# Chunk solves of a gated DeltaNet layer moved out of the step-by-step recurrence, output products in a stream of their own, PSUM banks shared anew

## The chip, the core and the metric

The kernel runs on one core of a Trainium2 chip. The metric is the device time of one execution in microseconds (us), from profiled or timed runs. TensorE (PE) multiplies into PSUM, eight banks of 128 x 512 float32; VectorE (DVE) and ScalarE (ACT) read PSUM; GpSimd (POOL) works on SBUF alone; SyncE (SP) issues the DMAs. Each engine takes its instructions in the order in which the program put them into its queue.

## The reference, cut to what matters

A block of two layers over 512 tokens (256 context, 256 latent), width 2048. Layer 0 is a bidirectional chunked gated DeltaNet, layer 1 differential attention. The part of layer 0 that is changed, for every head, direction and chunk:

```python
lower = jnp.where(strict, jnp.einsum('nbhid,nbhjd->nbhij', kb, kc) * decay, 0.0)
tinv = lax.linalg.triangular_solve(eye + lower, ...)          # per chunk
u = tinv @ (vc * bc[..., None])
w = tinv @ (kb * jnp.exp(gc)[..., None])
a_intra = jnp.einsum('nbhid,nbhjd->nbhij', qc, kc) * decay

def step(s, inp):
    q_i, k_i, u_i, w_i, a_i, gl_i = inp
    v_new = u_i - w_i @ s
    o_i = q_i @ s + a_i @ v_new
    s = s * gl_i[..., None, None] + jnp.einsum('bhck,bhcv->bhkv', k_i, v_new)
    return s, o_i
```

The kernel takes chunks of 128 tokens: four chunks (two of context, two of latent tokens), 32 value heads in 16 groups of two heads that share a key head, two directions.

## The kernel before

Layer 0 projects the normalised tokens to q, k, two v and two z tiles for each group g: six projections of 16 x 3 matmuls (three, because each float32 operand is split into a high part and a low part). A projection's weights come as four DMAs of 256 KB into `raw` tiles (four buffers), are split by ACT (`hi`) and POOL or DVE (`lo`) in `split` (L185, L187), and the products gather in a `pj` bank. The names in the traces say which: `g6z0hi` is the high part of group 6, first z projection.

The rest of layer 0 runs beside these projections. A planner written in the kernel (`Drive`, L497) holds a set of streams, Python generators, each with a priority, and lets the first one that is ready emit its next instructions; a stream says how much TensorE time it has just emitted and how long its result will take, and waits for events (`ev`) or for counted resources (`res`: `pj` 2, `kT` 3, `qT` 3, `v` 3, `m` 4, `uf` 8, `at` 3, and so on). The projections are the `filler`, with the lowest priority. The streams are:

- `stream_m`: per group and half (two chunks) the matrix of the triangular system in float16 plus a bfloat16 rest (`m16`, `ml`), and the inverse of its 16 x 16 diagonal blocks on DVE (`block_inv`);
- `stream_lev` (two): three levels that join the blocks into `uf`, an approximate inverse per chunk, by chains `iv` matmul, `R` on DVE (L783), `iv` matmul, `T` and `U` on ACT (L800, L801);
- `stream_at`: the masked, decayed scores `at`;
- `stream_b`: the recurrence, four steps per group, each with both directions and both heads. A step (`steps_b`, L849 to L933) multiplies the state with the keys (`sb` from `S` and `kT`), forms `y` on DVE (L874), casts it (L879), applies `uf`, casts (L898), multiplies by `m16` and `ml`, forms the rest on DVE (L905), applies `uf` again and adds (L911): that is the solve of the chunk with one refinement. Then come the new state (`sb` from `x` and `kx`, L918 or L921) and the outputs (`so` from `S` and `qT`, `so` from `x` and `at`), and `chain_fin` normalises and transposes the outputs of a half.

The eight PSUM banks are `pj` 2, `tr` 1, `iv` 2, `gq` 1, `sb` 1, `so` 1. On POOL and ACT runs besides the work on the modulation weights (`ada_pieces`: `rp` on L138, L139), fed by the DMAs `aw` and `cr`. After the streams follow the output projection in two halves (`woA`, `woB`), layer 1 (`dv`, `dk`, `dq`, `dg`) and its output projection (`dwo`), which use the same `raw` tiles; the products for q and the gate (`dq`, `dg`) and `dwo` have 256 columns, the others 512.

Of the kernel before, what the change touches and what calls it, by code (L numbers as in the profile page):

```python
# [20 lines left out]
P = 128  # L21
# [40 lines left out]
def body(ctx, tc, D, d, out):  # L62
# [87 lines left out]
    def ada_pieces(lcs):  # L150
# [3 lines left out]
        for q in range(NQ):  # L154
            yield
            cr = wp.tile([P, 2, NK], F32, name=f"cr{lcs[0]}{q}", tag="cr", bufs=2)
# [71 lines left out]
    sc_d = dram.tile([2, D], F32, name="sc_d")  # L228
    mb_d = [dram.tile([8, US], F16, name=f"mb_d{i}") for i in range(2)]
# [22 lines left out]
    gq = lambda: pt_("gq", 1)  # L252
# [4 lines left out]
    def so():  # L257
        return psm.tile([P, 2, 2, P], F32, tag="so", name="so", bufs=1)
# [37 lines left out]
    for k0 in range(0, KT, SK):  # L296
        with tc.high_priority():
            for kind in range(2):
                if k0 + kind:
                    pr = kind * HKT + k0 // 2  # L300
                    ada_pair(0, pr, ada_load(0, pr, t0, "ar", 12), (gq, tr)[np_ % 2](), t0)
                np_ += 1
# [24 lines left out]
    lv = cst.tile([P, 3, P], F32, name="lv")  # L327
    nc.sync.dma_start(lv, d["consts"][:, C_LV + 4 * P:C_LV + 7 * P].rearrange("p (l i) -> p l i", l=3))
# [27 lines left out]
    zt = dl.tile([P, 1024], F16, name="zt", tag="m16", bufs=4)  # L356
# [9 lines left out]
    hh = lambda kt: hhi[:, kt, :]  # L366

# [7 lines left out]
    def gates():  # L375
        class t1:
            @staticmethod
            def tile(shape, dt, name, tag, bufs=2):
                return dl.tile(shape, dt, name="gt_" + name, tag=tag, bufs=dict(at=3, x=1, cy=1, jk=1, y=1, grm=1, gra=1, ma=1).get(tag, bufs))
# [53 lines left out]
        g = t1.tile(sh, F32, name="g", tag="x")  # L433
# [121 lines left out]
    def post_k(g, ps):  # L555
# [8 lines left out]
        kT = dl.tile([P, NCH, P], F32, tag="kT", name=f"kT{g}", bufs=3)  # L564
        kt_ = dl.tile([P, NCH, P], F32, tag="ktok", name=f"ktok{g}", bufs=3)
        pt = tr()
# [9 lines left out]
        for c in range(NCH):  # L576
            nc.scalar.activation(kt_[:, c], pt[:, c * P:(c + 1) * P], AF.Copy, scale=rk[:, c:c + 1])
        yield 0.87, 6.0 * LX
        pt2 = tr()
# [3 lines left out]
        sts[g].update(kT=kT, ktok=kt_)  # L583
        yield 0.87, 1.5 * LX
        dr.set("kT", g)

    def post_q(g, ps):
# [13 lines left out]
        yield 0.0, 9.0 * LX  # L601
        pq = tr()
# [5 lines left out]
        dr.set("rq", g)  # L608
        yield 0.85, 0.0
# [13 lines left out]
    def post_v(g, h, ps):  # L623
        if h == 0:
            yield ("v", 2)
            sts[g]["v"] = [dl.tile([P, 2, 2, P], F32, tag="v", name=f"v{g}{i}", bufs=3) for i in range(2)]
# [9 lines left out]
        v = sts[g]["v"]  # L636
        pv = tr()
# [4 lines left out]
        for i in range(2):  # L642
            nc.scalar.activation(v[i][:, :, h, :], pvv[:, 2 * i:2 * i + 2], AF.Copy, scale=0.5)
        yield 0.87, 2.0 * LX
# [47 lines left out]
    def scaled(o, gr, pg, s, nm):  # L692
        gm = dl.tile([P, 2, P], F32, tag="gm", name=f"gm{s}{nm}", bufs=1)
        nc.vector.tensor_tensor(gm, pg.unsqueeze(1).to_broadcast([P, 2, P]), gam[:, s], ALU.mult)
# [3 lines left out]
    def block_inv(g, half, m16):  # L698
# [8 lines left out]
        TU = dl.tile([64, 2, 16, 16], F16, tag="bT", name=f"bT{nm}", bufs=1)  # L707
# [15 lines left out]
    def stream_m():  # L723
        for g in range(G):
            yield ev("kT", g)
            kT = sts[g]["kT"]
            for half in range(2):
# [6 lines left out]
                m16 = dl.tile([P, 2, 2, 2, P], F16, tag="m16", name=f"m16{nm}", bufs=4)  # L734
                ml = dl.tile([P, 2, 2, 2, P], BF16, tag="ml", name=f"ml{nm}", bufs=4)
                pg = gq()
                for k in range(2):
                    c = 2 * half + k
                    mm(pg[:, k * P:(k + 1) * P], kT[:, c], kT[:, c])
                for k in range(2):  # L740
# [3 lines left out]
                    scaled(ma, gr, pg[:, k * P:(k + 1) * P], 0, f"{g}{c}")  # L744
# [7 lines left out]
                free("gq", 1, 14)  # L752
                yield 0.44, 12.0 * LX

    def stream_lev(p):
        yield ev("conv", 0, "v0")
        yield ev("conv", 0, "v1")
        for g in range(G):
            for half in range(2):
# [17 lines left out]
                for n in range(4, 7):  # L777
# [10 lines left out]
                    if last:  # L788
                        uf = dl.tile([P, 4, P], F16, tag="uf", name=f"uf{g}{c}", bufs=8)
# [14 lines left out]
    def stream_at():  # L804
        for g in range(G):
# [4 lines left out]
            for half in range(2):  # L810
# [3 lines left out]
                for k in range(2):  # L814
                    c = 2 * half + k
                    mm(pg[:, k * P:(k + 1) * P], st["kT"][:, c], st["qT"][:, c])
                for k in range(2):
# [3 lines left out]
                    scaled(at, gr, pg[:, k * P:(k + 1) * P], 1, f"{g}{c}")  # L821
                    st["at"][c] = at
                dr.set("at", g, half, lat=8.0 * LX)
                free("gq", 1, 14)
                yield 0.44, 8.0 * LX

    def stream_b():
        if "k1" in early:
            yield ev("conv", 1, "k")
        for g in range(G):  # L830
            st = sts[g]
            for h in range(2):
                yield ev("v", g, h)
            S = dl.tile([P, 2, 2, P], F32, tag="S", name=f"S{g}", bufs=1)
            for half in range(2):
                for k in range(2):
                    yield ev("uf", g, 2 * half + k)
                O = dl.tile([P, 2, 2, P], F32, tag="O", name=f"O{g}{half}", bufs=2)
                for t in (2 * half, 2 * half + 1):
                    yield from steps_b(g, t, half, st, S, O)  # L840
                free("m")
                free("uf", 2)
                free("v")
                free("at", 2)
                dr.add(2, chain_fin(g, half, O))
            free("kT")
            free("qT")

    def steps_b(g, t, half, st, S, O):  # L849
        kT, qT, ktok, uf = st["kT"], st["qT"], st["ktok"], st["uf"]  # L850
        v = st["v"][half]
        m16, ml = st["m"][half]
        cd = (ORDER[0][t], ORDER[1][t])
        col = lambda a, dd, h: a[:, cd[dd], dd, 2 * g + h:2 * g + h + 1]
        fl = lambda a: a.rearrange("p d h i -> p (d h i)")
        f2 = lambda a: a.rearrange("p h i -> p (h i)")
        DH = [(dd, h) for dd in range(2) for h in range(2)]

        def vec(tag, dt=F32):
            return dl.tile([P, 2, 2, P], dt, tag=tag, name=f"{tag}{g}{t}", bufs=1)  # L860
# [7 lines left out]
        if t > 0:  # L868
            b = sb()
            for dd in range(2):  # L870
                mm(f2(b[:, dd]), kT[:, cd[dd]], f2(S[:, dd]))
            y = vec("y")
            for dd, h in DH:
                nc.vector.scalar_tensor_tensor(y[:, dd, h], b[:, dd, h], col(eg, dd, h), v[:, cd[dd] % 2, h],  # L874
                                               ALU.mult, ALU.subtract)
        else:
            y = v
        yb = vec("yb", BF16)
        nc.scalar.copy(fl(yb), fl(y))  # L879
        if t > 0:  # L880
            o1 = so()
            for dd in range(2):
                mm(f2(o1[:, cd[dd] % 2]), qT[:, cd[dd]], f2(S[:, dd]))
            for dd, h in DH:
                c = cd[dd] % 2
                if t == 2:
                    nc.scalar.activation(O[:, c, h], o1[:, c, h], AF.Copy, scale=col(eg, dd, h))
                else:
                    nc.vector.scalar_tensor_tensor(O[:, c, h], o1[:, c, h], col(eg, dd, h), O[:, c, h],
                                                   ALU.mult, ALU.add)  # L890
# [404 lines left out]
```

## Time and profile before

| what | value |
|---|---|
| median of three timed runs | 3165.09 us (3162.82 to 3166.16) |
| the profiled execution, its own time | 3170.24 us |
| its span, first to last instruction | 3168.5 us |
| TensorE busy, share of the span | 89% |
| VectorE, ScalarE, GpSimd busy | 62%, 59%, 64% |
| mean granted clock of TensorE | 0.954 of full speed |

A busy share is an average over stages: start-up to about 240 us, the streams of layer 0 beside the projections to about 2060 us, the output projection to about 2440 us, then layer 1. A matmul's time in the trace reaches from its start to its modelled end, and matmuls overlap; the distance from start to start tells what one costs in a dense row.

### The profile page before, as it was taken

To read this page: it belongs to the slowest core of one execution; us is meant where nothing else is said; L and a number is where in the kernel's file an instruction comes from. 1 tells how busy PE (TensorE), PEld (TensorE's weight loads), DVE (VectorE), ACT (ScalarE), POOL (GpSimd) and SP (SyncE) were. 2 spreads that over 40 slices of the span, in tenths; PEclk is the share of its full clock that TensorE was granted. 3 is DMA by queue.
4 is the path that set the end of the run, shared out by engine and by line. 5 is a ranking of instruction groups with operands and counts; after the bars stand their busy time and mean duration, and the time that the engine had idled before them with its cause. 6 is when DMAs were issued, how large, how long until landed. Compare 5 with 4: busy or idle time off the path is not lost.

```text
span 3168.5 us, 52448 instructions
## 1 busy us (share of the span) xinstructions
PE 2833.0 (89%) x16178; PEld 2236.6 (71%) x16178; DVE 1980.1 (62%) x4274; ACT 1863.0 (59%) x5466; POOL 2026.2 (64%) x2370
## 2 busy tenths in 40 slices
PE   4977888888998988998988988899898999999998
PEld 1555666676776766776766766677686888888888
DVE  2148768778778688588688688632334664545454
ACT  3545666666766766766666666654455665434354
POOL 2567677777787777777777777566466677322234
PEclk6988999999999999999999999999999999999999
DMA  9645445455545555545455546656744454333345
GB/s 362 223 114 118 123 119 135 123 133 118 139 134 129 127 126 133 128 129 136 122 125 131 132 118 134 173 171 189 230 147 132 144 164 150 123 110 113 117 127 164
DMA packets 511795, 457.06 MB, mean 144 GB/s; under 512 B 241684, under 2 KB 383764, under 8 KB 511508
## 3 DMA queue, kind: packets, MB, share of 16 engines
q1 hardware_dynamic: 511508, 453.68, 51.8%
q8 instruction: 127, 2.08, 0.3%
q14 instruction: 156, 1.28, 0.1%
q10 hardware_dynamic: 4, 0.02, 0.0%
HBM read 427.18 MB, written 26.36 MB: 143 GB/s over the span
## 4 chain that ended last, share of the span: by engine, by line
PE 33%; DVE 26%; DMA 19%; ACT 7%; POOL 7%; issue 5%; SPq 2%; POOLq 0%; DVEq 0%; ACTq 0%
PE pj L83 28%; DMA gra<-gc_d 5%; POOL rp L138 4%; DMA grm<-gc_d 4%; DVE bP L712 4%; DVE grm L687 3%; DMA aw<-in_adaw_dram 3%; DVE gra L687 2%; DVE bY L714 2%; ACT rp L139 2%; DVE R L783 1%; PE sb L83 1%; DMA ar<-in_adaw_dram 1%; PE iv L83 1%; DVE ma L695 1%
## 5 line engine op out<-in xcount | busy, mean ns | idle before, releaser
L139 ACT ACTIVATE rp<-rp 128x256 f32<-128x256 f32 x1024 | 426.9, 417 | 378.6 <-POOL rp L138 375.5
L712 DVE TENSOR_TENSOR bP<-bX,bY 64x1 f32<-64x1 f32 (+14 forms) x480 | 228.8, 477 | 18.1 <-ACT bY L710 9.8
L139 ACT ACTIVATION_READ_ACCUMULATOR rp<-rp 128x1 f32 x1024 | 194.0, 189 | 0.0
L687 DVE TENSOR_SCALAR gra<-gra,gct,lnb 128x128 f32<-128x128 f32 x256 | 114.3, 488 | 97.9 <-DMA gra<-gc_d 97.2
L687 DVE TENSOR_SCALAR grm<-grm,gct,lnb 128x128 f32<-128x128 f32 x256 | 144.9, 610 | 47.9 <-DMA grm<-gc_d 47.3
L783 DVE TENSOR_TENSOR R<-iv,lv 128x512 f16<-128x512 f32 x192 | 126.1, 678 | 32.8 <-PE iv L83 32.6
L689 ACT ACTIVATE grm<-grm 128x512 f32<-128x512 f32 x64 | 40.4, 631 | 132.0 <-DVE grm L687 127.1
L83 PEld LDWEIGHTS <-m 128*128 128x128 f16 x1024 | 74.2, 100 | 62.0 <-issue 57.7
L714 DVE TENSOR_REDUCE bY<-bP 64x1 f32<-64x1 f32 (+14 forms) x480 | 108.8, 227 | 8.7
L83 PE MATMUL iv<-U,R 128*128 128x128 f16 x768 | 75.7, 223 | 34.4 <-DVE R L783 30.0
L83 PEld LDWEIGHTS <-R 128*128 128x128 f16 x768 | 47.6, 99 | 77.6 <-DVE R L783 44.6
L745 POOL TENSOR_TENSOR ma<-ma,cs 128x512 f32<-128x512 f32 x64 | 85.3, 1333 | 20.7 <-DVE ma L695 18.3
L83 PE MATMUL sb<-yb,uf 128*128 128x128 bf16 x512 | 54.2, 225 | 40.7 <-ACT yb L879 22.2
L689 ACT ACTIVATE gra<-gra 128x512 f32<-128x512 f32 x64 | 40.4, 631 | 84.1 <-DVE gra L687 84.1
L83 PE MATMUL iv<-T,m 128*128 128x128 f16 x768 | 71.4, 223 | 15.8 <-ACT T L800 7.2
L224 DVE TENSOR_TENSOR hlo<-mh,hhi 128x512 fp32r<-128x512 f32 x32 | 29.6, 929 | 86.8 <-ACT hhi L223 77.8
L748 POOL TENSOR_TENSOR ml<-ma,m 128x512 bf16<-128x512 f32 x64 | 76.1, 1189 | 10.5 <-ACT m L747 10.3
L83 PEld LDWEIGHTS <-uf 128*128 128x128 f16 x512 | 36.4, 100 | 64.6 <-issue 59.1
L801 ACT CAST U<-iv 128x512 f16<-128x512 f32 x128 | 75.7, 591 | 0.0
L800 ACT CAST T<-iv 128x512 f16<-128x512 f32 x128 | 73.7, 576 | 3.0 <-PE iv L83 2.9
L83 PE MATMUL so<-x,at 128*128 128x128 f32 x512 | 71.6, 280 | 3.8 <-DVE x L911 2.7
L83 PEld LDWEIGHTS so<-x,at 128*128 128x128 f32 x512 | 64.9, 194 | 6.2 <-DVE x L911 3.6
(2758 smaller groups left out, 11429.3 us busy)
## 6 DMA issues: line engine op xcount, KB each, us to landing
aw<-in_adaw_dram SPq DMA_DIRECT2D x512, 128.0 KB, 3.0
ar<-in_adaw_dram SPq DMA_DIRECT2D x64, 512.0 KB, 7.3
gra<-gc_d SPq DMA_DIRECT2D x128, 128.0 KB, 4.2
grm<-gc_d SPq DMA_DIRECT2D x128, 128.0 KB, 4.1
mb_d<-m SPq DMA_DIRECT2D x32, 256.0 KB, 3.7
T<-tu_d SPq DMA_DIRECT2D x128, 64.0 KB, 2.7
U<-tu_d SPq DMA_DIRECT2D x128, 64.0 KB, 2.7
yd<-sz SPq DMA_DIRECT2D x32, 256.0 KB, 3.4
```

The costliest lines, as they stand in the source:

```text
L83: nc.tensor.matmul(o, l, r, start=start, stop=stop)
L138: nc.gpsimd.tensor_tensor(pr, r, cr[:, s], ALU.mult)
L139: nc.scalar.activation(pr, pr, AF.Copy, accum_out=acc[:, s, q:q + 1])
L687: nc.vector.tensor_scalar(gr[:, u], gr[:, u], gct[:, c, dd, j:j + 1], lnb[:, c, dd, j:j + 1], ALU.subtract, ALU.min)
L689: nc.scalar.activation(gr, gr, AF.Exp)
L712: nc.vector.tensor_tensor(pr[:, :i, :i], X[:, i, :i].unsqueeze(1).to_broadcast([64, i, i]), Y[:, :i, :i].rearrange("p j c -> p c j"), ALU. ...
L714: nc.vector.tensor_reduce(Y[:, i, :i], pr[:, :i, :i], AX.X, ALU.add)
L745: nc.gpsimd.tensor_tensor(ma, ma, ident.unsqueeze(1).to_broadcast([P, 4, P]), ALU.add)
L748: nc.gpsimd.tensor_tensor(ml[:, :, k], mv, m16[:, :, k], ALU.subtract)
L783: nc.vector.tensor_tensor(R, quad(pp), lvb(n), ALU.mult)
L800: nc.scalar.copy(Tm, quad(pt))
L801: nc.scalar.copy(U, quad(pu))
```

## The change

The solve of a chunk is applied to the values and to the decayed keys before the recurrence, as the reference writes it. `stream_v` makes `U` (the reference's `u`) for each chunk, `stream_w` makes `W`, the transposed `w`, for the steps that have a state (of the first two chunks only one direction each). Both run the same three passes as the old step (`uf`; `m16` and `ml`; `uf` again); the last pass of `stream_w` uses the data as weights, so that the result comes out transposed (a matmul with an identity `idh`, one with `uf`). A step of `stream_b` is left with `W` times `S`, the subtraction from `U`, and the new state. `stream_o` makes the outputs.

PSUM: `gq` is gone, its users take the one `tr` bank; `so` has two buffers, and is used by `stream_v`, `stream_w`, `stream_o` and `chain_fin`; each `so` and `tr` use is now a counted resource of the planner. To make room in SBUF several buffer counts fall: `raw` 4 to 3, `cr` 2 to 1, `kT` 3 to 2, `v` 3 to 2, `m16` and `ml` 4 to 3, `uf` 8 to 4. The mask products of two chunks become one instruction (`masked`).

```diff
-        r = wp.tile([P, 512], F32, tag="raw", name=nm, bufs=4)
+        r = wp.tile([P, 512], F32, tag="raw", name=nm, bufs=3)
...
+    MB, VB, UFB, UB, WB, CRB = 3, 2, 4, 2, 3, 1
...
-    gq = lambda: pt_("gq", 1)
+    gq = tr
...
-    res = {k: Res(n) for k, n in dict(pj=2, th=2, kT=3, qT=3, v=3, sz0=2,
-                                      sz1=2, gq=1, m=4, uf=8, at=3).items()}
+    res = {k: Res(n) for k, n in dict(pj=2, th=2, kT=2, ktok=3, qT=3, v=VB, sz0=2,
+                                      sz1=2, gq=1, m=MB, uf=UFB, at=3, U=UB, W=WB, so=2).items()}
...
+    def masked(pg, s, nm):
+        gm = dl.tile([P, 2, 2, P], F32, tag="gm", name=f"gm{s}{nm}", bufs=1)
+        nc.vector.tensor_tensor(gm, pg[:, :2 * P].rearrange("p (k i) -> p k i", k=2).unsqueeze(2).to_broadcast([P, 2, 2, P]),
+                                gam[:, s].unsqueeze(1).to_broadcast([P, 2, 2, P]), ALU.mult)
...
+    def stream_v():
...
+                    vb = dl.tile([P, 2, P], BF16, tag="vb", name=f"vb{g}{c}", bufs=1)
+                    nc.scalar.copy(vb, v[:, k])
...
+                    for dd, h in DH:
+                        mm(b[:, dd, h], uf[:, 2 * dd + h], vb[:, h])
+                    x0 = dl.tile([P, 2, 2, P], BF16, tag="x0", name=f"x0{g}{c}", bufs=1)
+                    nc.scalar.copy(x0, b)
...
+                        mm(b[:, dd, h], m16[:, dd, k, h], x0[:, dd, h], True, False)
+                        mm(b[:, dd, h], ml[:, dd, k, h], x0[:, dd, h], False, True)
+                    rb = dl.tile([P, 2, 2, P], BF16, tag="vb", name=f"rb{g}{c}", bufs=1)
+                    nc.vector.tensor_tensor(rb, v[:, k].unsqueeze(1).to_broadcast([P, 2, 2, P]), b, ALU.subtract)
...
+                        mm(b[:, dd, h], uf[:, 2 * dd + h], rb[:, dd, h])
+                    us = U[:, 0:4:3] if k == 0 else U[:, 1:3]
+                    nc.vector.tensor_tensor(us, x0, b, ALU.add)
...
+    def stream_w():
...
+                        nc.gpsimd.tensor_tensor(ek[:, i], ktok[:, c].unsqueeze(1).to_broadcast([P, 2, P]),
...
+                    nc.scalar.copy(eb, ek)
...
+                        mm(b[:, i, h], x0[:, i, h], idh, True, False)
+                        mm(b[:, i, h], rb[:, i, h], uf[:, 2 * dd + h], False, True)
+                    for i, dd in enumerate(dds):
+                        t = 2 * half + (k if dd == 0 else 1 - k)
+                        nc.scalar.copy(W[t][:, dd], b[:, i])
...
     def steps_b(g, t, half, st, S):
...
         if t > 0:
+            W = st["W"][t]
             b = sb()
             for dd, h in DH:
+                mm(b[:, dd, h], W[:, dd, h], S[:, dd, h])
+            nc.vector.tensor_tensor(x, x, b, ALU.subtract)
...
+    dr.add(1.3, stream_o())
+    dr.add(1.7, stream_v())
+    dr.add(1.6, stream_w())
```

How the instructions move. The first place is a step of the recurrence on TensorE: group 5, step 1 (`S5` or `S50` is the state after step 0). Before, these rows stand there, with 66 projection matmuls among them (left out, like repeated rows and the weight loads):

```order
L83 MATMUL sb_9923<-S5_9580,kT5_7820 128x256 x2
...
L83 MATMUL sb_9998<-yb51_9931,uf51_8932 128x128
...
L83 MATMUL so_9933<-S5_9580,qT5_8389 128x256 x2
...
L83 MATMUL sb_10030<-x051_10003,m1650_8084 128x128
...
L83 MATMUL sb_10071<-yb51_10039,uf51_8932 128x128
...
L83 MATMUL sb_10103<-x51_10076,kx51_9920 128x128 x4
```

Now, at the same step, with 12 projection matmuls among them:

```order
L83 MATMUL sb_10434<-S50_10384,W51_9056 128x128 x2
L83 LDWEIGHTS uf53_10158
L83 MATMUL so_10417<-eb53_10408,uf53_10158 128x128
...
L83 MATMUL iv_10965<-T60_10885,m1660_10297 128x128
...
L83 MATMUL so_10497<-xk53_10422,m1651_9133 128x128
...
L83 MATMUL sb_10515<-U50_9958,kx51_10431 128x128 x4
```

The three solve passes have left the step; passes of the `W` solve of another chunk (`eb53`, `xk53`) and of the next group's levels stand there instead.

The second place is TensorE where projection `g6z0` ends and `g6z1` begins. Before (`yb52` and `x052` belong to a solve, `T60` and `R60` to a level of the next group):

```order
L83 MATMUL pj_10568<-hhi_96,g6z0lo3256_10832 128x512
L83 MATMUL pj_10841<-hhi_96,g6z1hi00_10844 128x512
...
L83 MATMUL sb_10387<-yb52_10251,uf52_9416 128x128
...
L83 MATMUL pj_10841<-hhi_96,g6z1hi0256_10858 128x512
...
L83 MATMUL iv_10416<-T60_10363,m1660_9784 128x128
...
L83 MATMUL pj_10841<-hhi_96,g6z1hi10_10905 128x512
...
L83 MATMUL sb_10430<-x052_10392,m1651_8543 128x128
L83 MATMUL sb_10430<-x052_10392,ml51_8544 128x128
...
L83 MATMUL iv_10481<-U60_10364,R60_10421 128x128
...
L83 MATMUL pj_10841<-hhi_96,g6z1lo1256_10916 128x512
```

Now (each `iv` and `so` row stands four times; the rows with `x053` alternate, eight in all):

```order
L83 MATMUL iv_11102<-T60_11056,m1660_10297 128x128
...
L83 MATMUL iv_11109<-T61_11070,m1660_10297 128x128
L83 MATMUL pj_11353<-hlo15_1337,g6z0hi3256_11627 128x512
L83 MATMUL pj_11353<-hhi_96,g6z0lo3256_11628 128x512
...
L83 MATMUL iv_11154<-U60_11050,R60_11107 128x128
...
L83 MATMUL so_10704<-vb53_10702,uf53_10158 128x128
...
L83 MATMUL iv_11160<-R60_11107,U60_11050 128x128
...
L83 MATMUL so_10812<-x053_10709,m1651_9133 128x128
...
L83 MATMUL iv_11168<-U61_11064,R61_11114 128x128
...
L83 MATMUL so_10849<-rb53_10821,uf53_10158 128x128
...
L1089 MATMUL so_10875<-cs_63,O50_9835 128x128 x4
L83 MATMUL pj_11684<-hhi_96,g6z1hi00_11687 128x512
```

Where projections stood between the passes, 36 matmuls of the solve and of the levels now follow one another with none between.

## Rows read from the trace of the kernel before

**Rows 1.** The page's first part: busy time, share, instructions of each engine.

```profile
PE 2833.0 (89%) x16178; PEld 2236.6 (71%) x16178; DVE 1980.1 (62%) x4274; ACT 1863.0 (59%) x5466; POOL 2026.2 (64%) x2370
```

**Rows 2.** Windows by stage: length, busy PE, PEld, DVE, ACT, POOL, clock, DMA share, GB/s.

```profile
240.00:2060.00 1820.00, 1602.72 (x9379) 1235.40 (x9378) 1404.82 (x3222) 1194.10 (x3697) 1345.38 (x1657) 0.96 0.52 130
2700.00:3060.00 360.00, 354.67 (x2130) 311.57 (x2129) 182.23 (x362) 153.46 (x308) 109.06 (x89) 1.00 0.37 116
```

**Rows 3.** Timeline of TensorE in a dense row: start, length, engine, operation.

```profile
1043.97 0.22 PE L83 MATMUL sb<-x,m 128*128 128x128 bf16 x1
...
1044.25 0.22 PE L83 MATMUL sb<-x,ml 128*128 128x128 bf16 x1
...
1044.60 0.39 PE L83 MATMUL pj<-hhi,g8khi 128*128 128x512 f32 x1
1044.83 0.39 PE L83 MATMUL pj<-hlo,g8khi 128*128 128x512 f32 x1
```

**Rows 4.** Waits of TensorE from 240 to 2060 us: total, times, longest.

```profile
PE iv L83 <- DVE R L783: 31.6, 35, 3.7
PE sb L83 <- ACT yb L879: 22.2, 18, 3.6
PE sb L83 <- DVE yb L905: 18.3, 16, 3.6
PE gq L83 <- DVE gm L694: 16.8, 13, 2.6
...
PE sb L83 <- DVE x L911: 4.6, 4, 2.2
PE sb L83 <- DVE S L918: 3.9, 3, 2.1
```

**Rows 5.** Timeline of TensorE where solve passes follow without projections; waits in brackets.

```profile
2028.54 0.39 PE L83 MATMUL iv<-T,m 128*128 128x128 f16 x4
2031.17 0.38 PE L83 MATMUL sb<-yb,uf 128*128 128x128 bf16 x4 [2.25 <-ACT yb L879]
...
2033.62 0.27 PE L83 MATMUL sb<-x,m 128*128 128x128 bf16 x1 [0.95 <-ACT x L898]
```

**Rows 6.** Windows around a run of short waits of TensorE; columns as rows 2.

```profile
1985.00:1994.00 9.00, 6.88 (x42) 5.29 (x41) 4.02 (x13) 6.47 (x23) 4.69 (x6) 1.00 0.40 109
1994.00:2002.00 8.00, 7.58 (x28) 5.09 (x28) 3.13 (x5) 5.70 (x17) 4.98 (x8) 0.57 0.37 111
```

**Rows 7.** Groups of instructions, 240 to 2060 us: count, busy, mean ns, idle before.

```profile
L865 POOL TENSOR_TENSOR kx<-ktok,kd 128x256 f32<-128x256 f32 x94 | 63.4, 695 | 1.9 <-PE sb L83 1.2 <-DVE kd L458 0.7
...
L694 DVE TENSOR_TENSOR gm<-gq,cs 128x256 f32<-128x256 f32 x128 | 52.9, 413 | 6.0 <-PE gq L83 4.9
...
L874 DVE SCALAR_TENSOR_TENSOR y<-sb,eg,v 128x128 f32<-128x128 f32 x184 | 51.9, 338 | 4.1 <-PE sb L83 3.9
...
L879 ACT CAST yb<-y 128x512 bf16<-128x512 f32 x46 | 28.4, 618 | 20.8 <-DVE y L874 20.6
...
L643 ACT ACTIVATE v<-tr 128x256 f32<-128x256 f32 x64 | 21.6, 376 | 1.4 <-PE tr L639 1.3
```

**Rows 8.** DMA issues from 3060 us: size of each, median us to landing.

```profile
dwo5r<-in_dawo_dram SPq DMA_DIRECT2D x4, 256.0 KB, 3.9
```

**Rows 9.** Timeline of ACT, then of POOL and DVE, in the last projection.

```profile
3095.37 0.62 ACT L185 CAST dwo6hi<-dwo6r 128x512 fp32r<-128x512 f32 x1 [0.32 <-DMA dwo6r<-in_dawo_dram]
...
3096.07 1.30 POOL L187 TENSOR_TENSOR dwo6lo<-dwo6r,dwo6hi 128x512 fp32r<-128x512 f32 x1 [0.80 <-ACT dwo6hi L185]
...
3097.40 0.69 DVE L187 TENSOR_TENSOR dwo6lo<-dwo6r,dwo6hi 128x512 fp32r<-128x512 f32 x1
```

**Rows 10.** Timeline of TensorE in the same projection.

```profile
3095.44 0.28 PE L83 MATMUL pj<-yh,dwo5lo 128*128 128x256 f32 x1
3095.56 0.28 PE L83 MATMUL pj<-yh,dwo5hi 128*128 128x256 f32 x1
```

**Rows 11.** The page: DMA issues of the modulation weights, KB each, us to landing.

```profile
aw<-in_adaw_dram SPq DMA_DIRECT2D x512, 128.0 KB, 3.0
```

More of the change, by code (lines that the diff above doesn't have):

```diff
@@ L492, in ev, with done @@
         return evs.setdefault(k, Event())
-    res = {k: Res(n) for k, n in dict(pj=2, th=2, kT=3, qT=3, v=3, sz0=2,
-                                      sz1=2, gq=1, m=4, uf=8, at=3).items()}
+    res = {k: Res(n) for k, n in dict(pj=2, th=2, kT=2, ktok=3, qT=3, v=VB, sz0=2,
+                                      sz1=2, gq=1, m=MB, uf=UFB, at=3, U=UB, W=WB, so=2).items()}
+    cnt = {}
+    def done(what, key, n):
+        cnt[key] = cnt.get(key, 0) + 1
+        if cnt[key] == n:
+            free(what)
     class Drive:
@@ L583, in post_k @@
         sts[g].update(kT=kT, ktok=kt_)
+        free("gq", 1, 3)
         yield 0.87, 1.5 * LX
@@ L608, in post_q @@
         dr.set("rq", g)
+        free("gq", 1, 3)
         yield 0.85, 0.0
@@ L625, in post_v @@
             yield ("v", 2)
-            sts[g]["v"] = [dl.tile([P, 2, 2, P], F32, tag="v", name=f"v{g}{i}", bufs=3) for i in range(2)]
+            sts[g]["v"] = [dl.tile([P, 2, 2, P], F32, tag="v", name=f"v{g}{i}", bufs=VB) for i in range(2)]
             dr.set("vt", g)
@@ L751, in stream_m @@
                 dr.set("tu", g, half, lat=32)
-                free("gq", 1, 14)
                 yield 0.44, 12.0 * LX
+            done("kT", ("kT", g), 2)
     def stream_lev(p):
@@ L816, in stream_at @@
                     mm(pg[:, k * P:(k + 1) * P], st["kT"][:, c], st["qT"][:, c])
+                gm = masked(pg, 1, f"{g}{half}")
+                free("gq", 1, 4)
                 for k in range(2):
@@ L827, in stream_b @@
+    DH = [(dd, h) for dd in range(2) for h in range(2)]
     def stream_b():
@@ L831, in stream_b, with steps_b, vec @@
             st = sts[g]
[L832 to L852, printed above, removed]
+            st["S"] = {}
+            S = None
+            for t in range(4):
+                half = t // 2
+                if t % 2 == 0:
+                    yield ev("U", g, half)
+                    yield ev("W", g, half)
+                S = yield from steps_b(g, t, half, st, S)
+            free("ktok")
+    def steps_b(g, t, half, st, S):
+        ktok = st["ktok"]
         cd = (ORDER[0][t], ORDER[1][t])
         col = lambda a, dd, h: a[:, cd[dd], dd, 2 * g + h:2 * g + h + 1]
[L855 to L860, printed above, removed]
+        x = st["U"][half][:, t % 2:4:2]
+        def vec(tag, dt=F32, bufs=1):
+            return dl.tile([P, 2, 2, P], dt, tag=tag, name=f"{tag}{g}{t}", bufs=bufs)
         if t < 3:
@@ L880, in steps_b @@
[L880 to L890, printed above, removed]
-            yield 1.7, 2.6 * LX
-        else:
-            yield 0.0, 1.0 * LX
+                mm(b[:, dd, h], W[:, dd, h], S[:, dd, h])
@@ L962, in chain_fin @@
                                            sz[h][:, sl], ALU.mult, ALU.mult)
+        free("so", 1, 3.5)
         yield 0.87, 1.0
```

240 lines of the change are left out of this document (175 added, 65 removed).

## The prediction

> **What bounds the kernel now.** I read the page's engine shares first: TensorE 89%, no other engine above 64% [rows 1]. A matmul's busy time overlaps its neighbours', so I then read the windows and the timeline. In the stage of the streams, 240 to 2060 us, TensorE is busy for 1602.7 of 1820 us, and the reader is to see two things: 217 us lie idle, and the granted clock is 0.96 on average [rows 2]. The timeline shows that busy is nearly full here: in a dense row the 128-column bfloat16 matmuls start 0.056 us apart (six starts from 1043.97 to 1044.25) and the 512-column ones 0.23 us apart [rows 3]. So what is added to TensorE's queue is added to the time, unless it falls into the 217 us. The list of waits says what those are: the level chain's `R` costs 31.6 us; the solve inside the recurrence costs 22.2 + 18.3 us (`yb`), 4.6 us (`x`) and 3.9 us (`S`), together 49; `gq` waits 16.8 us for the mask product [rows 4]. The rest is spread over weight splits and others. The recurrence is therefore not what paces this stage; it takes 49 us of 1820 from TensorE, because projections stand between its passes.
>
> **The change, part by part.** The sum is made against the profiled execution's 3170.2 us, which is 5.1 us above the median of the runs.
>
> *Added matmuls.* `stream_v` has the passes that the recurrence had (16 matmuls a chunk). `stream_w` is new: 10 matmuls in each of a group's first two chunks and 20 in the other two, 60 a group, 960 in all. `W` times `S` has the columns of `kT` times `S` in twice as many instructions. 960 x 0.056 us = 54 us [rows 3]. Below: nothing, if all fell into the idle 217 us. Above: at half the clock twice as much, 108 us. I take 54, since a pass in order pushes back whatever is behind it. By the Trainium skill's page "TensorE: Matmul & The Clock Gate", section "Back-to-back issue gap", a sustained stream of weight load and matmul pairs takes about 81 ns a matmul at 128 columns; the trace shows 56 ns, and the sum would be 78 us by the page instead of 54.
>
> *Stretches without projections.* This is the largest term. In the new order the planner finds no projection to emit once in nearly every group: as I read the code, `v` and `kT` have two buffers instead of three, so the results that occupy the two `pj` banks wait until the last chunk's solve is done, and the next projection waits for the bank. The second place of the listings shows it: between `g6z0` and `g6z1` stand 36 matmuls of solves and levels, each pass fed by the one just before through DVE or ACT; before, projections stood there. What such a hop costs uncovered: from the first matmul of one solve pass (2031.17) to the first of the next (2033.62) 2.45 us, with little work between; the pass before it waited 2.25 us [rows 5]. In the piece shown, `vb53` to `x053` has 8 small matmuls under it (0.44 us), so 2.0 us are lost; `x053` to `rb53` has 16 (0.9), so 1.6; `T60` to `R60` has 8 and three projection matmuls (1.1), so 1.3. Together 4.9 us for 36 matmuls. Counted over the whole order, the stage has 20 stretches of 28 or more matmuls without a projection, 1250 matmuls in all (five of them with over 100, the longest 276, after `g1z1`); before, one, with 40. At 4.9 us for 36 that is 170 us. In the long ones two level chains and both solves cover one another, so I take 110. Below: one uncovered hop in each stretch, 20 x 2.0 = 40 us; above: 170.
>
> *Clock.* After a run of short waits the granted clock stood at 0.57 over 8 us, after a window at full clock (so 1.2 instead of 2.4 GHz for most of it): 0.43 x 8 = 3.4 us [rows 6]. For 20 stretches that is at most 68 us, at least nothing; the waits in most stretches are short, so I take 15.
>
> *What the recurrence gives back.* Its 49 us and the 16.8 us of `gq`, 66 in all [rows 4]. The same passes now stand in `stream_v` and again in `stream_w`, so not all of it goes: I take 30; bounds 0 and 66.
>
> *Other engines.* ACT loses 64 casts `yb` (618 ns) and gains 64 `vb` and 96 copies to `W` of 256 columns (376 ns, as `v`), and 64 each of `eb` and `xk`, half of them of 512 columns (618) and half of 256: -40 + 60 + 64 = +84 us. POOL gains 96 `ek` (as `kx`, 695 ns): +67 us. DVE loses 192 `y` (338) and half of 128 `gm`, and gains 48 subtractions, 64 `rk` and wider masks: within 10 us of nothing [rows 7]. ACT has 626 us free in the stage and POOL 475 [rows 2], so I cost this at nothing; they split the weights too, and where a split comes late TensorE waits, for which the high side holds 40 us.
>
> *Buffers of weights.* A `raw` tile of `dwo` lives 3.9 us until the DMA has landed, 0.62 us for `hi` and 0.69 (DVE) or 1.30 us (POOL) for `lo`, 5.5 us on average [rows 8, 9]. ACT already waits for the DMA there [rows 9]. With four buffers a tile can come every 1.4 us; its 12 matmuls of 256 columns take 12 x 0.12 = 1.44 us [rows 10]. With three it comes every 1.84 us: 0.40 x 64 tiles = 26 us. The 128 tiles of `dq` and `dg` would lose 51 us, but each run of 16 tiles starts with up to six prepared ones (8.6 us of work against 6.4 lost), so I take 10 of them: 36 us; bounds 0 (fewer DMAs at once may land sooner) and 77. That stage has no slack, busy 354.7 of 360 us [rows 2]. The projections of 512 columns use a tile in 2.8 us (12 x 0.23) and don't feel it. `cr` with one buffer makes POOL wait for one landing a piece (3.0 us for `aw` [rows 11], 128 pieces); this work is off the path and I cost it at nothing; SP's later DMAs, `raw` among them, stand behind that wait, which belongs to the 40 us above. Sharing `gq` with `tr` and giving `so` a second buffer I cost at nothing of their own: their waits are part of the stretches.
>
> Sum: 54 + 110 + 15 - 30 + 36 = +185 us; 3170.2 + 185 = 3355, beside the median 3350. With every bound at its low end it is -26 (40 - 66), with every one at its high end over +460.
>
> **Rivals.**
> - *The stretches cost nothing* because the engines, freed of backlog, answer at once: 54 of matmuls, less 30, and a little for the buffers: about 3190 to 3225. For it: outside such places a hop's 2.45 us holds time in which ACT did other casts. Against: each stretch still has serial passes. It decides if a hop costs under 1 us.
> - *The recurrence did pace the stage.* The place is the `sb` chain; the price is its 66 us of waits, the 31.6 of `R`, and the clock that the waits cost (0.04 x 1820 = 73): -170 + 54 = -116, about 3050. It decides if the waits that vanish exceed 54 plus whatever the new stretches cost. For it: the busy share counts overlapping time. By the Trainium skill's page "Perfetto Trace Analysis", section "Identifying the Most-Contended Engine", a matmul busy share says little about how near TensorE is to its limit, and the weight-load share should be read; that is 68% here (1235 of 1820 us), which would leave room. Against: the dense starts of rows 3, and that the listing has the projections taken out of the places where they covered passes.
> - *Nothing measurable:* the passes fall into idle time and the stretches cancel the relief; 3159 to 3171.
> - *Weights late as well:* `cr` waits on SP and the added ACT and POOL work hold the splits back in the streams' stage: 185 + 77 - 36 + 40 and the upper bound of the stretches, over 3470.
>
> **How the numbers follow.** Main course 0.64 (3225 to 3470); stretches free 0.12 (slower too); recurrence pace 0.14 (faster); nothing 0.04; weights late 0.06 (slower). So faster 0.14, within 0.2% 0.04, slower 0.82; 0.2%, some 6 us, is what a measurement of this kernel can tell from no change. The range 3160 to 3470 leaves out the faster case and the late weights, 0.20; given the main course alone it is 3225 to 3470. The predicted time is 3350.
>
> **What would show it.** In the profile after: TensorE's instruction count up by about 960 and their pairs of weight loads; in the streams' stage more idle time on TensorE than 217 us, with waits for `R`, `x0`, `rb` and `T` named, in bunches of 5 to 20 us where `z0` ends and `z1` begins; a longer stretch after `g1z1`; granted clock below 0.96 there; `dwo` projections waiting for `hi` or `lo` with ACT waiting for the DMA. I would be wrong if the stage grew by little more than 54 us, or shrank: then the hops in the stretches are cheaper than 2.45 us, or waits that I put down to others hung on the recurrence.

## The result, and the profile after

| kernel | median | ratio to before, 95% interval |
|---|---|---|
| before | 3164.05 us | |
| changed | 3475.91 us (3474.34 to 3479.53) | 1.0987 [1.0967, 1.1006] |

The change costs 312 us. 185 were forecast, and the range ended at 3470. The page of the changed kernel has more matmuls and lower shares on every engine than [rows 1]: nothing became a bound by being busy, every engine waits more.

```profile
PE 2977.3 (86%) x17330; PEld 2344.5 (67%) x17330; DVE 1983.2 (57%) x4130; ACT 1925.8 (55%) x5692; POOL 2048.8 (59%) x2466
```

To see where, cut both executions at the same places of the program: last projection of layer 0 done, `woB7` done, first start of `dwo0`, end. Windows of before, then of the changed kernel; columns as in rows 2.

```profile
240.00:2009.00 1769.00, 1561.41 (x9118) 1203.15 (x9117) 1366.07 (x3139) 1158.60 (x3600) 1319.18 (x1628) 0.96 0.51 128
2009.00:2345.00 336.00, 313.72 (x1429) 244.23 (x1428) 126.45 (x252) 174.99 (x523) 195.09 (x216) 0.96 0.65 191
2345.00:3053.00 708.00, 684.65 (x3811) 588.16 (x3810) 361.11 (x688) 368.86 (x934) 344.61 (x335) 0.99 0.43 131
3053.00:3169.00 116.00, 99.87 (x820) 96.37 (x818) 56.37 (x101) 50.75 (x96) 48.66 (x38) 0.96 0.52 156
```

```profile
240.00:2215.00 1975.00, 1660.72 (x10100) 1287.01 (x10100) 1340.56 (x2929) 1217.95 (x3821) 1352.79 (x1736) 0.93 0.46 115
2215.00:2601.00 386.00, 343.11 (x1563) 256.67 (x1563) 150.34 (x292) 188.45 (x559) 203.71 (x221) 0.92 0.58 167
2601.00:3347.00 746.00, 698.54 (x3810) 591.61 (x3809) 355.25 (x687) 348.77 (x860) 313.15 (x299) 0.98 0.43 120
3347.00:3478.00 131.00, 105.94 (x822) 97.55 (x820) 58.37 (x103) 50.34 (x97) 48.33 (x38) 0.96 0.49 141
```

The stages grew by 206, 50, 38 and 15 us. The first is the streams' stage, where the forecast put everything but the weights' term. But 103 us lie behind it: 50 in the output projection of layer 0, beside which the last streams run, and 53 behind `woB7`, where none of the new streams runs and, of what is priced below, only the buffer counts are left of the change. In the first stage TensorE's idle time went from 208 (1769 less 1561) to 314 us and its busy time up by 99; a matmul counts longer at a lower clock (0.63 us instead of 0.39 for 512 columns, from 1010 to 1013 us, where the granted clock is 0.50), and the granted clock went from 0.96 to 0.93. The waits of TensorE there (240 to 2300 us; answers to [rows 4]): `yb` is gone and `gm` down to 2.2 us, but `R` grew and the solves' waits stand in `so` instead of `sb`, once for the values (`rb`, `vb`) and once for the keys (`rk`).

```profile
PE iv L83 <- DVE R L810: 47.4, 41, 4.6
PE so L83 <- DVE rb L888: 35.5, 21, 4.8
PE so L83 <- DVE rk L943: 20.7, 15, 2.6
PE iv L83 <- ACT T L827: 20.6, 20, 2.9
PE iv L83 <- DMA T<-tu_d: 20.4, 28, 1.9
PE so L83 <- ACT vb L870: 15.3, 4, 6.4
```

The forecast stretches are there. For each of the 89 projections from `g1q` on, take the first and the last start of a product of two high parts (`hhi` with a `hi` tile). The times from one projection's last to the next one's first add up to 372 us, before to 78; the projections themselves take 1628 against 1709, since less stands between their matmuls. This is the one between `g6z0` and `g6z1`, TensorE's timeline with waits in brackets, and then a window of it with the columns of rows 2:

```profile
1029.61 0.39 PE L83 MATMUL pj<-hhi,g6z0lo 128*128 128x512 f32 x1
1034.60 0.61 PE L83 MATMUL iv<-U,R 128*128 128x128 f16 x4 [4.59 <-DVE R L810]
...
1037.59 0.59 PE L83 MATMUL iv<-R,U 128*128 128x128 f16 x4
1040.99 0.59 PE L83 MATMUL so<-rb,uf 128*128 128x128 bf16 x4 [2.81 <-DVE rb L888]
1041.37 1.06 PE L1089 MATMUL so<-cs,O 128*128 128x128 f32 x4
1042.08 0.78 PE L83 MATMUL pj<-hhi,g6z1hi 128*128 128x512 f32 x1
```

```profile
1035.00:1041.00 6.00, 2.97 (x27) 2.60 (x26) 4.67 (x10) 3.88 (x10) 4.19 (x6) 0.50 0.64 155
```

`g6z1` starts 0.5 us after the last tap of the convolution `cyg7k`, which frees its bank. The projection `g7k` had ended near 1004, so the bank waited over 30 us for VectorE, whose timeline has the four taps between solves, and waits of its own for transfers:

```profile
1034.46 0.73 DVE L478 SCALAR_TENSOR_TENSOR cyg7k<-pj,convw,cyg7k 128x508 f32<-128x508 f32 x1
1035.12 0.68 DVE L810 TENSOR_TENSOR R<-iv,lv 128x512 f16<-128x512 f32 x1
1035.71 0.73 DVE L478 SCALAR_TENSOR_TENSOR cyg7k<-pj,convw,cyg7k 128x510 f32<-128x510 f32 x1
1037.74 1.95 DVE L708 TENSOR_SCALAR grm<-grm,gct,lnb 128x128 f32<-128x128 f32 x4 [1.29 <-DMA grm<-gc_d]
1039.61 0.73 DVE L478 SCALAR_TENSOR_TENSOR cyg7k<-pj,convw,cyg7k 128x510 f32<-128x510 f32 x1
1040.27 0.67 DVE L888 TENSOR_TENSOR rb<-v,so 128x512 bf16<-128x512 f32 x1
1040.86 0.73 DVE L478 SCALAR_TENSOR_TENSOR cyg7k<-pj,convw,cyg7k 128x508 f32<-128x508 f32 x1
```

What the forecast did not price stands on GpSimd, a little earlier, in its timeline and then in ScalarE's:

```profile
1006.86 2.10 POOL L187 TENSOR_TENSOR g6z0lo<-g6z0r,g6z0hi 128x256 fp32r<-128x256 f32 x3 [0.37 <-POOL kx L989]
1014.33 0.72 POOL L138 TENSOR_TENSOR rp<-aw,cr(1, 4)0_22991 128x256 f32<-128x256 f32 x1 [5.37 <-DMA cr(1, 4)0_22991<-sc_d]
1015.67 0.73 POOL L138 TENSOR_TENSOR rp<-aw,cr(1, 4)0_22991 128x256 f32<-128x256 f32 x1 [0.62 <-ACT rp L139]
1016.36 0.72 POOL L187 TENSOR_TENSOR g6z0lo<-g6z0r,g6z0hi 128x256 fp32r<-128x256 f32 x1
```

```profile
1007.71 0.59 ACT L879 CAST x<-so 128x512 bf16<-128x512 f32 x1
1015.08 0.42 ACT L139 ACTIVATE rp<-rp 128x256 f32<-128x256 f32 x1 [6.78 <-POOL rp L138]
1015.41 0.19 ACT L139 ACTIVATION_READ_ACCUMULATOR rp<-rp 128x1 f32 x1
1015.50 0.39 ACT L185 CAST g6z0hi<-g6z0r 128x256 fp32r<-128x256 f32 x1
```

GpSimd stands 5.4 us until the one `cr` buffer is filled again, ScalarE 6.8 us for GpSimd's product, and the weights of `g6z0` stand behind both. In this place TensorE had other work and did not wait; how long it does wait for weights in all is in the next section. Before, no wait for `cr` is listed; here 103 waits with 242 us are (added over all rows of this kind).

### The profile page after: what moved, and what is told of

It is laid out like the page before. It is cut to its first block, busy times and chain, and to the rows that moved or that the text cites. A ratio compares the mean times of both kernels' runs of the same rounds, so it can differ in the third digit from the quotient of the medians.

```text
span 3477.7 us, 55150 instructions
## 1 busy us (share of the span) xinstructions
PE 2977.3 (86%) x17330; PEld 2344.5 (67%) x17330; DVE 1983.2 (57%) x4130; ACT 1925.8 (55%) x5692; POOL 2048.8 (59%) x2466
## 5 line engine op out<-in xcount | busy, mean ns | idle before, releaser
L139 ACT ACTIVATE rp<-rp 128x256 f32<-128x256 f32 x1024 | 427.8, 418 | 652.5 <-POOL rp L138 649.1
L708 DVE TENSOR_SCALAR grm<-grm,gct,lnb 128x128 f32<-128x128 f32 x256 | 136.5, 580 | 111.8 <-DMA grm<-gc_d 111.5
L708 DVE TENSOR_SCALAR gra<-gra,gct,lnb 128x128 f32<-128x128 f32 x256 | 107.3, 463 | 138.7 <-DMA gra<-gc_d 138.2
L83 PEld LDWEIGHTS <-m 128*128 128x128 f16 x1216 | 100.2, 104 | 86.1 <-issue 76.5
L83 PE MATMUL iv<-T,m 128*128 128x128 f16 x768 | 81.8, 231 | 33.8 <-DMA T<-tu_d 20.4
L83 PEld LDWEIGHTS <-uf 128*128 128x128 f16 x704 | 51.1, 104 | 87.4 <-issue 73.8
L920 POOL TENSOR_TENSOR ek<-ktok,eg 128x256 f32<-128x256 f32 x96 | 63.0, 670 | 25.7 <-DVE rk L943 20.9
L83 PE MATMUL so<-U,at 128*128 128x128 f32 x512 | 70.3, 282 | 2.2 <-DVE rk L943 0.9
L83 PEld LDWEIGHTS so<-U,at 128*128 128x128 f32 x512 | 66.0, 198 | 5.6 <-DVE rk L943 1.3
```

The costliest lines, as they stand in the source:

```text
L83: nc.tensor.matmul(o, l, r, start=start, stop=stop)
L139: nc.scalar.activation(pr, pr, AF.Copy, accum_out=acc[:, s, q:q + 1])
L708: nc.vector.tensor_scalar(gr[:, u], gr[:, u], gct[:, c, dd, j:j + 1], lnb[:, c, dd, j:j + 1], ALU.subtract, ALU.min)
L920: nc.gpsimd.tensor_tensor(ek[:, i], ktok[:, c].unsqueeze(1).to_broadcast([P, 2, P]), eg[:, c, dd, 2 * g:2 * g + 2].unsqueeze(2).to_broadca ...
```

## The experiments

Prices are differences of medians to the kernel before of the same comparison (3161 to 3166 us), or to the changed kernel.

**One buffer of `cr` alone**, in the kernel before.

```diff
-            cr = wp.tile([P, 2, NK], F32, ..., tag="cr", bufs=2)
+            cr = wp.tile([P, 2, NK], F32, ..., tag="cr", bufs=1)
```

> The kernel before with one cr buffer instead of two, nothing else. Theory V (the prediction's: two buffers of v and kT hold the projections up) and theory P (the added passes themselves cost it): cr is off the path, 3160 to 3180 us. Theory S (with one cr buffer SyncE waits 145 us for GpSimd's rp before each cr transfer, and gra, grm and raw behind it land late, so that VectorE's queue and with it the convolutions that free the pj banks run late): 3230 us or more, the wait of gra and grm for their transfers up from 144 us towards the 249 us of the changed kernel.

3282.49 us, 1.0373 [1.0353, 1.0394]: 118 us. But theory S named the wrong path: the waits for `gra` and `grm` are 101.5 and 49.9 us, hardly above before (97.2 and 47.3). Two of the 96 waits of GpSimd for `cr`, 240 us in all, between 1800 and 2700 us, from its list of waits:

```profile
POOL rp L138 <- DMA cr(1, 24)7_27696<-sc_d: 5.2, 1, 5.2
POOL rp L138 <- DMA cr(1, 36)0_31416<-sc_d: 5.0, 1, 5.0
```

ScalarE's wait for `rp` over the whole span of this kernel, 375.5 us before:

```profile
ACT rp L139 <- POOL rp L138: 639.6, 573, 7.6
```

The weights come late with it: TensorE's waits for the halves of a projection's weights (all rows from a `pj` matmul to a `hi` or `lo` tile of L185 or L187, added) are 129 us, before 70. So 59 of the 118 us show there; where the others arise was not followed. By place, 37 us of the profiled execution's growth lie in the streams' stage, 18 in the output projection of layer 0 and 57 between `woB7` and `dwo0`.

**Two buffers of `v` and `kT`**, in the kernel before.

```diff
-    res = ... kT=3, qT=3, v=3, ...
+    res = ... kT=2, qT=3, v=2, ...     (and bufs=2 of the tiles)
```

> The kernel before with v and kT in two buffers instead of three, nothing else; in it the projections stand still in 6 stretches of 28 or more matmuls (428 in all) instead of 1 (40), at the boundary from z1 to the next q. Theory V: 3250 us or more. Theory S and theory P: under 3215 us, since the stretches before had 13.6 us for 36 matmuls only where the convolutions ran late.

3216.04 us, 1.0168 [1.0151, 1.0185]: 52 us. Its order has 388 more matmuls in stretches; that is 0.134 us each, against 4.9 / 36 = 0.136 in the prediction. Its trace, counted between two projections, has 468 more, and 39 us of the profiled execution's growth lie in the streams' stage; that would be 0.08. The median is 1 us above what theories S and P allowed and far from theory V. The times between projections grow from 78 to 150 us.

**Four buffers of `v`**, in the changed kernel.

```diff
-            ... dl.tile([P, 2, 2, P], F32, tag="v", ..., bufs=VB)    # VB = 2
+            ... dl.tile([P, 2, 2, P], BF16, tag="v", ..., bufs=VB)   # VB = 4
```

> The changed kernel with v kept as bfloat16, so that four buffers of v fit in the place of two (v is rounded). Theory V: the stretches between z0 and z1 lose their cause, 3380 us or less. Theories S and P: 3440 to 3500 us.

3441.77 us, 1.0881 [1.0864, 1.0897]: 34 us less than the changed kernel. 11 stretches of 28 or more matmuls between two projections, 1036 matmuls in all, stay in its trace (in the changed kernel 14 with 1236), and 320 us of times between projections. No run has `v` in bfloat16 alone, so what the type gives is not known; it stands in the next run too.

**Two buffers of `cr`**, in the changed kernel (`v` as above, but `VB = 2`, `CRB = 2`).

> The changed kernel with v kept as bfloat16 in two buffers (v is rounded) and a second cr buffer in the room that this leaves. Theory S: SyncE's wait of 145 us at cr goes, 3380 us or less. Theories V and P: 3440 to 3490 us.

3368.71 us, 1.065 [1.0634, 1.0666]: 107 us less. GpSimd's waits for `cr` are 7 us, ScalarE's for `rp` 415.9 (649.1 in the changed kernel), TensorE's for the halves of weights 73 (118 there).

**`cr` from another queue**, in the changed kernel.

```diff
-                nc.sync.dma_start(cr[:, s], sc_d[...])
+                nc.scalar.dma_start(cr[:, s], sc_d[...])
```

> The changed kernel with the cr transfers issued from ScalarE's queue, still one buffer. If the harm of the one buffer is SyncE's waiting (145 us at cr), with aw, raw, gra and grm queued behind it: 3400 us or less, as with the second buffer (3369). If the harm is that the modulation work itself waits for each landing, or if ScalarE's queue is held up instead: 3440 to 3520.

3473.98 us, 1.0971 [1.094, 1.1001]: nothing gained. SyncE's 145 us at `cr` are gone; GpSimd's waits for the landing (90, 221 us) and ScalarE's for `rp` are not:

```profile
ACT rp L139 <- POOL rp L138: 628.0, 557, 5.6
```

SyncE is little freed by this, as most of its wait for the same products of GpSimd moves to the next `aw` (over the span 662 us, and 759 at `aw` and `cr` in the changed kernel). But it stands as long at `aw` in the kernel with two buffers of `cr` (639 us), which is 105 us faster. So it is not the standing of SyncE's queue that carries the price. It goes with GpSimd's wait for the landing.

**All buffer counts of the change**, in the kernel before (`raw` 3, `cr` 1, `kT` 2, `v` 2, `m16` and `ml` 3, `uf` 4).

> The kernel before with all buffer counts of the changed one (raw 3, cr 1, kT 2, v 2, m16 and ml 3, uf 4), the solves still in the recurrence. If the smaller buffers cost most of the 312 us, and their prices add (cr 118, v and kT 52, raw about 20, m and uf not yet priced): 3350 us or more. If the new passes and their order cost most: under 3350, since cr, v and kT together make 170.

3363.19 us, 1.0621 [1.0596, 1.0647]: 198 us, most of the 312, with the solves still in the recurrence.

**The PSUM part alone**, in the kernel before.

```diff
-    gq = lambda: pt_("gq", 1)
+    gq = tr            # and masked(), the gq waits of the posts, so bufs=2, bT in bP's buffer
```

> The kernel before with the PSUM part of the change alone: gq shares the one tr bank, counted by the planner, so has two buffers, the two mask products are one, bT shares bP. If the banks matter: 3190 us or more, since every transpose and score product waits for one bank. If they don't, and the merged mask product (64 fewer instructions on VectorE, and the bank free after it) gives a little: 3140 to 3180.

3172.16 us, 1.0025 [1.001, 1.0041]: 7 us.

**Without the solve of `W`**, in the changed kernel (`W` is a copy of `ek`).

```diff
-                    (three passes: eb, xk, rk; 960 matmuls)
-                        nc.scalar.copy(W[t][:, dd], b[:, i])
+                        nc.scalar.copy(W[t][:, dd], ek[:, i])
```

> The changed kernel without the solve of W: W is a copy of the decayed keys, 960 matmuls with their copies and subtractions are left out. If the added matmuls cost their issue time (960 x 56 to 81 ns, 54 to 78 us): 3395 to 3425. If their serial hops make much of the stretches: under 3380. If they lie under others' waits: over 3440.

3345.77 us, 1.0564 [1.0543, 1.0586]: 130 us less. The stretches go with it, although `v` and `kT` still have two buffers: the times between projections add up to 110 us instead of 372, 41 of these after `g1z1`, and of the 14 stretches 4 are left, one of them with 260 of their 348 matmuls. The granted clock of the streams' stage is 0.96 again.

**The same matmuls without their hops.**

```diff
-   x0 = copy(b); rb = ek - b      (between the passes)
+   all passes in one go, on eb
```

> The changed kernel with all 960 matmuls of W's solve, but none waits for another: the three passes of a chunk stand in one go on eb, the copies xk and the subtractions rk between them are left out, so W is not the solve. Beside the kernel without the solve (3346): if the matmuls' issue time is most of the 130 us that the solve costs, 3420 us or more (54 to 78 us over it); if the hops between the passes, that wait for ScalarE and VectorE in the middle of TensorE's queue, are most, 3400 us or less.

3436.75 us, 1.0873 [1.0847, 1.0899]: 91 us over the kernel without the solve, and 39 us under the changed one, which is the price of the hops by subtraction. The 91 us are 95 ns for each of the 960 matmuls, but the matmuls themselves take less. One chunk's last passes in this run's timeline of TensorE, eight starts in 0.39 us:

```profile
999.79 0.22 PE L83 MATMUL so<-idh,eb 128*128 128x128 bf16 x1
999.85 0.22 PE L83 MATMUL so<-uf,eb 128*128 128x128 f16 x1
...
1000.18 0.22 PE L83 MATMUL so<-uf,eb 128*128 128x128 f16 x1
```

Over the streams' stage the 900 of them that the trace has take 59 ns on average from start to start, waits left out, so an estimate for all is 57 us. The other 34 us come with them: the stretches are back (342 us between projections against 110), and TensorE's idle time in the stage is 297 us (240 to 2187.6) against 252 (240 to 2075.4) without the solve. This run also has the 64 casts to `eb` that the one without the solve leaves out; the order and these casts were not separated. In the changed kernel's groups of TensorE (240 to 2215 us; count, busy, mean ns, idle before) the hops show as waits of the last pass:

```profile
L83 PE MATMUL so<-idh,xk 128*128 128x128 bf16 x180 | 28.2, 221 | 8.5 <-DVE rk L943 6.8 <-DVE O L1057 0.9 <-DVE O L1045 0.8
L83 PE MATMUL so<-xk,m 128*128 128x128 bf16 x180 | 27.2, 222 | 0.5 <-ACT xk L934 0.4
...
L83 PE MATMUL so<-uf,rk 128*128 128x128 f16 x180 | 26.9, 220 | 12.9 <-DVE rk L943 12.9
```

**Three `raw` tiles**, in the kernel before.

> The kernel before with three raw tiles instead of four, nothing else. The prediction's term was 36 us, from the output projection of layer 1 (26) and the 256-column projections (10): 3195 to 3205. If only the output projections feel it, as the profiles of the changed kernel with a second cr buffer show (13 us over the kernel before there, 8 in the first half of the output projection of layer 0): 3175 to 3190.

3212.55 us, 1.0155 [1.0133, 1.0177]: 51 us, more than either expectation. Its profiled execution is 46 us longer than that of before: 17 from `dwo0` to the end, 18 from `woB7` to `dwo0`, 12 earlier.

**Three buffers of `m16` and `ml`, four of `uf`**, in the kernel before.

> The kernel before with three buffers of m16 and ml instead of four and four of uf instead of eight. The prices of cr (118), v and kT (52) and raw (51) add up to 221 and all counts together cost 198: if prices add, this one is -23, 3140; if they overlap, 3160 to 3190.

3199.26 us, 1.0108 [1.0092, 1.0125]: 33 us, more than either expectation. 20 of the 32 us by which its profiled execution grew lie in the output projection of layer 0. The single prices, 118 + 52 + 51 + 33 = 254, overlap by 56.

**Without the solve of `W`, with `cr` 2 and `raw` 4**, in the changed kernel.

> The changed kernel without the solve of W (W is a copy of the decayed keys), with v kept as bfloat16 (rounded), and in the room that this leaves a second cr and a fourth raw tile. If the books close (312 = buffers 198 + banks 8 + solve of W 130 - 24 for what the recurrence gives back), what is left is v, kT, m and uf with 29, the banks and the -24: 3165 to 3195. If the emptied recurrence gives more once the weights come in time: under 3155. If another cost of the new streams is hidden in the parts: 3210 or more.

3224.04 us, 1.0189 [1.0172, 1.0206], 58 us over before. With `m` and `uf` now at 33, what is left in it is 52 + 33 + 7 = 92; the emptied recurrence would give back 34. That the expectation had 3165 to 3195 comes from `m` and `uf`, taken as -23 by subtraction.

**More buffers for the modulation work**, in the kernel before: two `rp`; two `rp` and three `aw` (`bT` in `bP`'s buffer for the room); three `aw`; and, as control, what made room for them (`lv` in float16) alone.

```diff
-        pr = wp.tile([P, NK], F32, tag="rp", ..., bufs=1)
+        pr = wp.tile([P, NK], F32, tag="rp", ..., bufs=2)
...
-        r = wp.tile([P, NK], F32, tag="ra", name=f"aw...", bufs=2)
+        r = wp.tile([P, NK], F32, tag="ra", name=f"aw...", bufs=3)
```

> The kernel before with two rp buffers instead of one (room from lv in float16), nothing else. GpSimd waits 308 us for ScalarE's accumulate to free the one rp. If idle time of GpSimd ahead of the weight splits is what the cr buffer's price was made of, less of it makes the kernel faster: 3120 to 3155. If GpSimd has enough time at rp, 3155 to 3175.

> As the kernel with two rp buffers, and three aw buffers instead of two (bT shares bP for the room). SyncE waits 349 us for GpSimd before aw transfers, and GpSimd 73 us for their landing. If these waits hold up the weights behind them, 3100 to 3150; if not, as with two rp buffers alone.

> The kernel before with three aw buffers instead of two (room from lv in float16), rp stays at one. If GpSimd's waits for a landing, with the weight splits behind them in its queue, are what costs time (cr: 240 us of such waits more and 118 us of time more), then without the 73 us for aw: 3125 to 3150. If instead any faster progress of the modulation work takes GpSimd from the weights (as two rp buffers, 76 us slower, may have done): 3175 to 3240.

> The kernel before with lv in float16 alone, as the kernel with the third aw buffer has it. If the 32 us that this one gained come from the third buffer: 3155 to 3175. If they come from lv: 3140 or less.

| kernel | median | ratio | GpSimd waits for `aw`, us |
|---|---|---|---|
| two `rp` | 3237.58 | 1.0244 [1.0227, 1.0261] | 148.9 |
| two `rp`, three `aw` | 3183.32 | 1.0069 [1.0049, 1.0088] | 41.9 |
| three `aw` | 3134.57 | 0.9905 [0.9891, 0.992] | 4.8 |
| `lv` alone | 3153.13 | 0.9964 [0.9953, 0.9975] | 54.6 |

Both kernels with two `rp` missed what was expected of them. Three `aw` buffers make the fastest kernel of all, 32 us under before; 11 of them come from `lv`, which the control shows. Its GpSimd still waits for ScalarE, more than before (308 us), and that costs nothing visible:

```profile
POOL rp L138 <- ACT rp L139: 370.0, 361, 4.0
```

## Why the prediction was wrong

**The step that failed** is, in the prediction's words: "`cr` with one buffer makes POOL wait for one landing a piece ...; this work is off the path and I cost it at nothing". The wait is real (103 of them, 2.4 us on average) and costs 118 us in the kernel before, 107 in the changed one (there with `v` in bfloat16). The modulation work is off the path, but it stands in GpSimd's and ScalarE's queues between the splits of the weights and the casts of the chains. A landing that GpSimd waits for stops both engines, and the halves of the weights come late: TensorE's waits for them go from 70 to 129 us with one `cr` in the kernel before, and from 118 to 73 with two in the changed one. The runs agree on the order of the size: 209 us more of such waits (`cr` +240, `aw` -31) cost 118; 50 us fewer (54.6 to 4.8) gave 19 over the control. That SyncE's queue spreads it, as the prediction's reserve of 40 us had it, the run with `cr` from ScalarE's queue contradicts. Of what grew behind the streams' stage, one `cr` alone makes 75 us in the kernel before and three `raw` alone 42, and the two overlap. The rival "weights late as well", over 3470 at a chance of 0.06, has the number that came. Its mechanism was right about the weights, wrong about the queue and far too small in price (40 us), and it got over 3470 by the upper bound of the stretches, so the number is in part luck.

A second term was left out without a reason: the prediction prices no loss for `m16`, `ml` and `uf`, which alone cost 33 us.

**Added matmuls:** forecast 54 (0 to 108), and the matmuls themselves take some 57: 59 ns each, near the 56 ns of the dense row. By the Trainium skill's page "TensorE: Matmul & The Clock Gate", section "Back-to-back issue gap", an estimate would be 78 us, from about 81 ns; this case's traces do not agree with it. What the term missed is that the solve costs 130 us and not its matmuls alone: 39 are the hops, and 34 come with the order that the planner makes of it and with the casts to `eb`.

**Stretches:** forecast 110 (40 to 170) with `v` and `kT` as cause. They cost 52 alone, but most of the stretches of the changed kernel have another cause: without the solve of `W`, and `v` and `kT` still at two, the gaps between projections are 110 us instead of 372. With its matmuls but without its hops they are 342, so it is the second solve's place in the planner's order that opens them, not its hops. Nor is a gap lost time of its own: to close 262 us of them and to leave out 960 matmuls gave 130 us together, since the matmuls in a gap would stand elsewhere. The best sum that the runs allow is 52 for `v` and `kT`, 39 for the hops and 34 for the order, 125, with prices that overlap; that it lies near 110 is in part luck, for the price of a hop was misread. Before the 2.25 us wait of rows 5, ScalarE stood for a landing of weights, and the next pass waited for three casts of `yr`; this is ScalarE's timeline there:

```profile
2029.99 0.62 ACT L185 CAST woA0hi<-woA0r 128x512 fp32r<-128x512 f32 x1 [2.81 <-DMA woA0r<-in_wout_dram]
2030.51 0.61 ACT L879 CAST yb<-v 128x512 bf16<-128x512 f32 x1
...
2031.44 1.64 ACT L185 CAST yh<-yr 128x512 fp32r<-128x512 f32 x3
2032.99 0.57 ACT L898 CAST x<-sb 128x512 bf16<-128x512 f32 x1
```

So the row that priced the stretches already showed what one `cr` buffer does: an engine's wait for a landing stops the work behind it. The hops of `W`'s solve cost 39 us for two in each of 64 chunks, 0.3 us each over covered and uncovered ones; the forecast had 1.3 to 2.0 for an uncovered one. In the stretch shown it is VectorE's late convolutions that hold the bank, not `v`; why VectorE is late there (solve passes, transfers, ScalarE) was not separated.

**Clock:** 15 us (0 to 68). The granted clock of the streams' stage fell by 0.03, by estimate at most 59 us of 1975. In the stretch shown it was 0.50 (1.2 GHz) from 1035 to 1041 us, after TensorE had stood for 4.59 us. No run prices it by itself; without the solve of `W` the clock of the stage is 0.96, so the 130 us contain some of it.

**Relief of the recurrence:** forecast -30. 312 - 198 - 7 - 130 leaves -23, and the kernel without the solve and with more buffers -34. This is by subtraction, with prices that overlap; no run shows it by itself. The rival that the recurrence paced the stage needed 170, and the time moved the other way: it falls.

**Weights' buffers:** forecast 36 (0 to 77), measured 51. From `dwo0` on, 17 instead of 26; between `woB7` and `dwo0` 18 instead of 10; and 12 earlier, where the prediction had none.

**Other engines and banks:** "nothing of their own" holds for the banks (7 us).

In sum, buffers cost 198 of the 312, the second solve 130, the banks 7, and moving the solves out of the recurrence gave back 23 to 34. The rival of free stretches (3190 to 3225) and that of no measurable change fall with the time; against the first also stand the 52 us of `v` and `kT` and the 39 of the hops.

## What to carry to other kernels

Work that is off the path is not free if it shares an in-order queue with work on it: price its waits for a landing by what stands behind them on that engine, and on the engines that wait for it. When a change pays for space with buffer counts, run the old kernel with the new counts first; here that one run found two thirds of the loss. A stream added to a planner costs more than its matmuls: these came at the price of the dense row, 57 us, and the stream at 130. Leave it out in a copy of the kernel, and look at what it does to the order of the others.

## What was not expected of the hardware

Where GpSimd waits for a landing, each microsecond cost 0.4 to 0.6 us of the whole (118 / 209, 19 / 50), while 62 us more of waits for ScalarE (370.0 against 308.1) came with a faster kernel. And two `rp` buffers, which cut GpSimd's waits for ScalarE from 308 to 84 us, made the kernel 84 us slower than its control; its waits for `aw` doubled (148.9), but with three `aw` buffers, 41.9 us of them and 30 us over the control are left. Landings do not explain those 30; GpSimd and ScalarE are busier in the streams' stage there (1452 and 1219 us from 240 to 2000, against 1313 and 1154 before). But TensorE's waits for the halves of weights are 68 us there and 69 in the control, so that the faster modulation work takes the engines from the weights does not show; the cause stays open. With two `rp` alone these waits are 112 us.
